# Spreading a transformer's seam products over more PSUM banks, and taking cross attention's scores a head ahead

## Chip, cores and metric

The kernel runs on one core of a Trainium2 chip, whose TensorE (PE) multiplies matrices into eight PSUM banks of 128 partitions by 512 float32 columns; VectorE (DVE), ScalarE (ACT) and GpSimd (POOL) do the rest, and SyncE (SP) issues most loads. The metric is device microseconds (us) of one execution.

## What is computed

Two transformer blocks are run one after the other on x of 512 tokens by 1024 features, all in float32. The change touches only the second, which has two layers and a last norm:

```python
for l in range(DEPTH_2):                       # 2
    h = _rmsnorm(x, g_mix[l])
    (a_cq, a_ckv, a_kr, b_q, b_ff, b_fb, b_i, b_g,
     c_q, c_k, c_v, gate_a, gate_b, gate_c) = _split_cols(h @ w_in[l], IN_SPLITS_2)
    y_a = _mla(a_cq, a_ckv, a_kr, ...)         # 8 heads, low-rank q (384) and kv (256)
    y_b = _hgrn2(b_q, b_ff, b_fb, b_i, b_g, ...)   # gated recurrence, both directions
    y_c = _window_gqa(c_q, c_k, c_v, rel_bias, c_sink[l])
    merged = (jax.nn.sigmoid(gate_a) * (y_a @ w_br_a[l])
              + jax.nn.sigmoid(gate_b) * (y_b @ w_br_b[l])
              + jax.nn.sigmoid(gate_c) * (y_c @ w_br_c[l]))
    x = x + merged @ w_out[l]
    h = _rmsnorm(x, g_x[l])
    x = x + _cross(h, _rmsnorm(mem, g_mem[l]), x_wq[l], x_wkv[l], x_wo[l])   # 4 heads, 256 keys
    h = _rmsnorm(x, g_ffn[l])
    x = x + _swiglu(h, f_w1[l], f_w3[l], f_w2[l])   # 2816 wide
return _rmsnorm(x, g_final)
```

## The kernel before

Activations stand feature-first, 8 tiles of 128 features by 512 tokens. Each float32 product is made of three matmuls: both operands are split into a rounded part and a rest (`hi`, `lo`), and `mm3` adds hi x hi, hi x lo and lo x hi. `gemm_fm` (L390) is the common product: `wslab` (L380) loads a weight slab on SP's queue into `wraw` (two buffers), ACT writes `whi`, and POOL or DVE in turn writes `wlo` (three buffers each). Then 8 tiles of the inner dimension give 24 matmuls of 128x512 into one bank, which some instruction of DVE or ACT empties (it "evacuates" the bank): mostly a product with the row of norms, `r`. With an inner dimension of 1024 that is a product of 24 matmuls; the branches of the merge have 12, and the down projection of the feed-forward 66.

The eight banks are shared by four tags of two: g, s, t and o (`ps(tag)`, L312). A product of a tag waits until one of its two banks has been emptied. In the second half g takes all products of weights; s takes scores and the state products of the recurrence, t takes transpositions and sums over partitions, o takes outputs of attention and of the recurrence.

The order of the instructions on each engine is not that of the source: the program is built with a scheduler that runs it on a model of the engines (`TileContext(..., schedule_with_timeline_sim=True)`, L2742) and writes out, for each engine, a fixed list. It lets an instruction go ahead where its bank and its operands are free in the model. On the chip each engine goes through its list in order, and waits where an operand or a bank isn't ready.

A layer of the second half has these stages, each of which opens its own pools:

- norm: the row `rmix` (names `ssacc`, `rsv`, `rsr`, `rst` are steps of its inverse root).
- recurrence `hgrn`: `hgrn_values` makes the values `hv` in two halves of two banks, for which `rmix` is transposed to tokens; then 8 heads in two directions, each with products for q and z and a chain through state tiles (`h_S` on POOL, `h_qi`, `h_kx` and others). Its end makes a norm (`rsq`) and the branch's output, split into `ybh` and `ybl`.
- latent attention `mla`: `latent` makes two k tiles and three q tiles in `mraw`, norms them and splits them to `mlhk`, `mllk`, `mlhq`, `mllq`; then products with uk, uv and uq, the rope products `p1` and `p2`, and 8 heads, whose scores are already taken one head ahead. Output `yah`, `yal`.
- `window` attention: key `wk`, value `wvf`, four query products, 8 heads; output `ych`, `ycl`.
- 24 gate products (`gates2`, evacuated to `g2z` and stored in DRAM as `gated`) are strewn between the heads of the three branches by `beside` and `next(fill)`.
- `merge2`: the tiles of the gates are loaded (`g20`, `g21`, `g22` on SP), 8 x 3 branch products are multiplied with them, and 8 products with w_out follow.
- `cross` attention: for each of 4 heads two q products (`xq`), four score tiles with softmax, then transpositions and values; 8 products with x_wo.
- `ffn`: 22 pairs of products with f_w1 and f_w3 (`fz` is the first one's evacuation), then 8 products with f_w2.

The numbers behind a name (`ps_g_18632`) in the lists of the section on the change are serial numbers of the tiles; they are the same in both kernels. The functions that the diff touches, with the profile's line numbers:

## Time and profile before

| | us |
|---|---|
| median of 3 runs | 4423.25 (4420.15 to 4430.96) |
| the profiled execution | 4420.88, of which its span 4419.1 |
| first block | up to 1823 |
| layer 0: recurrence, latent attention | 1836 to 2161, to 2361 |
| layer 0: window, merge, cross, feed-forward | to 2494, 2616, 2740, 3111 |
| layer 1: recurrence, latent attention | 3111 to 3457, to 3658 |
| layer 1: window, merge, cross, feed-forward | to 3791, 3913, 4037, 4396 |
| last norm | to 4419 |

The bounds of the stages are read from the timeline, where the first product of the next stage begins. The span is cut into windows at such bounds, and each window tells how long every engine was busy in it and which clock the throttle granted to PE (1.00 is full speed, 2.4 GHz; 0.50 is 1.2 GHz). What a window has beyond PE's busy time is PE's idle time; the waits then say which engine's instruction ended that.

### The profile page before, as it was taken

The page shows a single profiled execution, that of the slowest core. Times are in us where ns is not written, and L with a number is a line of the kernel's source. Part 1 is how long each engine was busy: PE and PEld are TensorE (multiplying, and loading weights), DVE is VectorE, ACT ScalarE, POOL GpSimd, SP SyncE. Part 2 cuts the span into 40 slices and gives each one's busy share as a digit, 9 for nine tenths or more (in the row PEclk, how much of TensorE's full clock was granted, in tenths as well). Part 3 has the DMA queues.
Part 4 walks back from the last instruction along what each step waited for, and adds up shares of the span by engine and source line. Part 5 has one row for each costly group of instructions (what it writes and reads, how often), then busy time and mean ns, then how long its engine had stood idle before and what let it go on. Part 6 is the DMA issues. An engine that isn't in the chain of part 4 may idle for free. (4 is left out here: it accounts for less than half of the span.)

```text
span 4419.1 us, 55886 instructions
## 1 busy us (share of the span) xinstructions
PE 4036.6 (91%) x20436; PEld 3236.0 (73%) x20436; DVE 2728.1 (62%) x4770; ACT 2114.6 (48%) x3424; POOL 1692.5 (38%) x1144
## 2 busy tenths in 40 slices
PE   6999799869987989799899999999999899999998
PEld 4887676658866767678676777888777677777886
DVE  6657777677655778576566655332587475665542
ACT  4565668733332768433365544442344365444432
POOL 3342676523222353233254422332344264423431
PEclk8999899979978999899999999999999899999999
DMA  4432210034215889312131332223212122422232
GB/s 154 161 123 70 91 39 8 8 130 146 82 63 186 322 315 376 117 59 70 54 109 66 112 125 71 96 91 98 73 58 75 60 86 79 134 96 81 96 92 80
DMA packets 179605, 480.55 MB, mean 109 GB/s; under 512 B 17576, under 2 KB 28904, under 8 KB 178944
## 3 DMA queue, kind: packets, MB, share of 16 engines
q1 hardware_dynamic: 172512, 452.79, 30.0%
q0 software_dynamic: 6816, 24.15, 1.6%
q8 instruction: 163, 2.67, 0.2%
q14 instruction: 114, 0.93, 0.1%
HBM read 433.31 MB, written 41.44 MB: 107 GB/s over the span
## 5 line engine op out<-in xcount | busy, mean ns | idle before, releaser
L377 POOL TENSOR_TENSOR wlo<-wraw,whi 128x1024 fp32r<-128x1024 f32 (+4 forms) x244 | 554.9, 2274 | 1172.9 <-ACT whi L329 1118.0
L329 ACT ACTIVATE whi<-wraw 128x1024 fp32r<-128x1024 f32 (+4 forms) x489 | 481.7, 986 | 934.6 <-PE ps_g L317 746.6
L317 PE MATMUL ps_g<-ha,whi 128*128 128x512 f32 x2184 | 884.6, 405 | 48.3 <-DVE mraw L357 22.8
L317 PE MATMUL ps_g<-hl,whi 128*128 128x512 f32 x2184 | 887.5, 407 | 0.0
L317 PE MATMUL ps_g<-ha,wlo 128*128 128x512 f32 x2184 | 878.6, 403 | 0.0
L317 PEld LDWEIGHTS ps_g<-ha,whi 128*128 128x128 f32 x2184 | 417.5, 191 | 157.7 <-DVE mraw L357 22.3
L317 PEld LDWEIGHTS ps_g<-ha,wlo 128*128 128x128 f32 x2184 | 417.0, 191 | 100.2 <-issue 5.0
L317 PEld LDWEIGHTS ps_g<-hl,whi 128*128 128x128 f32 x2184 | 417.7, 191 | 97.6 <-issue 5.3
L377 DVE TENSOR_TENSOR wlo<-wraw,whi 128x1024 fp32r<-128x1024 f32 (+4 forms) x245 | 296.1, 1208 | 205.3 <-ACT whi L329 198.6
L353 DVE TENSOR_TENSOR_SCAN aa<-aa 128x774 f32<-128x774 f32 x64 | 126.1, 1971 | 51.1 <-ACT aa L329 46.8
L317 PE MATMUL ps_g<-fah,wlo 128*128 128x512 f32 x352 | 137.0, 389 | 0.0
L317 PE MATMUL ps_g<-fal,whi 128*128 128x512 f32 x352 | 137.0, 389 | 0.0
L317 PE MATMUL ps_g<-fah,whi 128*128 128x512 f32 x352 | 136.9, 389 | 0.0
L367 DVE SCALAR_TENSOR_TENSOR h_R<-h_R,h_gd,ps_s 128x64 f32<-128x64 f32 x448 | 124.7, 278 | 11.9
L329 ACT ACTIVATE aa<-ps_x,aM 128x512 f32<-128x512 f32 x128 | 110.8, 949 | 33.1 <-PE ps_x L317 21.0
L317 PE MATMUL ps_g<-mlo,xh 128*128 128x512 f32 x272 | 111.4, 409 | 14.2 <-POOL mlo L1946 14.2
L2347 POOL TENSOR_SCALAR mP<-mP,sfst 128x512 f32<-128x512 f32 x64 | 102.5, 1609 | 52.6 <-DVE sfst L2346 41.7
L2561 POOL TENSOR_SCALAR g2z<-g2z 128x512 f32<-128x512 f32 x48 | 81.9, 1706 | 95.0 <-DVE g2z L357 82.3
L1517 POOL TENSOR_TENSOR dnl<-dnn,dnc 128x512 f32<-128x512 f32 x48 | 67.1, 1408 | 125.6 <-PE ps_t L317 84.6
L329 ACT ACTIVATE g2z<-g2z 128x512 f32<-128x512 f32 x144 | 90.4, 628 | 49.7 <-POOL g2z L2561 48.1
L329 ACT ACTIVATE mhi<-mrawa 128x2048 fp32r<-128x2048 f32 x52 | 99.6, 1915 | 30.0 <-PE ps_g L317 11.2
L357 DVE TENSOR_TENSOR mlo<-mrawb,mhi 128x2048 fp32r<-128x2048 f32 x42 | 102.8, 2470 | 15.6 <-ACT mhi L329 15.6
(988 smaller groups left out, 10183.8 us busy)
## 6 DMA issues: line engine op xcount, KB each, us to landing
wraw<-w_fm SPq DMA_DIRECT2D x169, 512.0 KB, 3.4
wraw<-f_w SPq DMA_DIRECT2D x120, 512.0 KB, 3.5
mrawa<-moe_g SPq DMA_DIRECT2D x18, 1024.0 KB, 10.6
mrawb<-moe_d SPq DMA_DIRECT2D x18, 1024.0 KB, 8.3
adaw<-ada_w SPq DMA_DIRECT2D x64, 256.0 KB, 3.1
mrawa<-moe_u SPq DMA_DIRECT2D x16, 1024.0 KB, 9.3
mrawb<-moe_u SPq DMA_DIRECT2D x16, 1024.0 KB, 10.5
mrawb<-moe_g SPq DMA_DIRECT2D x14, 1024.0 KB, 10.4
```

Of the source, the lines that this page charges most:

```text
L317: self.nc.tensor.matmul(out, a, b, start=start, stop=stop)
L329: return self.nc.scalar.activation(out, in_, f, **kw)
L353: return self.nc.vector.tensor_tensor_scan(out, *args, **kw)
L357: return self.nc.vector.tensor_tensor(out, a, b, op=op)
L367: return self.nc.vector.scalar_tensor_tensor(out, a, s, b, op0=op0, op1=op1)
L377: e.tensor_tensor(lo, src, hi, op=OP.subtract)
L1517: nc.gpsimd.tensor_tensor(nl, n_, dnc[:, 1 + lv, None, :].to_broadcast([128, 4, 128]), op=OP.mult)
L2347: nc.gpsimd.tensor_scalar(P, P, st[:, 3:4], None, op0=OP.mult)
L2561: self.nc.gpsimd.tensor_scalar(z, z, ZMIN, None, op0=OP.max)
```

## The change

The tag of the products at the stages' seams is given by hand. `hgrn_values`: the second half of the values on s for g. `mla`: the k and q tiles of the latents on s, g, o in turn; uk, uv and uq products on g and s in turn; the two rope products on o. `window`: key and value on s, queries on g and s in turn. `merge2`: the three branches on g, s and t, w_out on g and s in turn. `ffn`: products with f_w3 on s, those with f_w2 on g and o in turn. In `cross` a head's q products, scores and softmax become a function, which is called for the next head ahead of a head's transpositions and values. No instruction is taken out or put in, except that one row of PE's list is split; the scheduler writes a new order for every engine.

```diff
--- before.py
+++ after.py
@@ -2166,7 +2166,7 @@
         rt = self.rows(T, r, 4, "rtok")
         v = T.tile([128, 4, 512], F32, name="hv")
         for hf in range(2):
-            pa = [self.ps("g"), self.ps("g")]
+            pa = [self.ps("gs"[hf]), self.ps("gs"[hf])]
             for c in range(2):
                 hi, lo = self.wslab(self.I["w2_i%d" % l][hf * 2 + c])
                 for kk in range(4):
@@ -2385,7 +2385,7 @@
                 def latent(n, at, gname, kt):
                     raw = T.tile([128, 3, S], F32, name="mraw", bufs=1)
                     for k in range(kt):
-                        self.tt(raw[:, k, :], self.gemm_fm(W2[at + k], self.ha, self.hl), r, OP.mult)
+                        self.tt(raw[:, k, :], self.gemm_fm(W2[at + k], self.ha, self.hl, tag="sgo"[k]), r, OP.mult)
                     yield 0.5
                     rs = self.rstd_x(T, raw, S, kt)
                     yield 0.5
@@ -2407,21 +2407,21 @@
                 self.tt(t[0:32], t[0:32], ropek[0:32], OP.mult)
                 self.tt(kr, t[0:32], t2, OP.add)
                 for n in range(4):
-                    self.act(kn[:, n, :], self.gemm_fm(I["a_uk%d" % l][n], kh, kl))
+                    self.act(kn[:, n, :], self.gemm_fm(I["a_uk%d" % l][n], kh, kl, tag="gs"[n % 2]))
                 yield 0
                 hi, lo = self.wslab(I["a_uv%d" % l])
                 for b in range(4):
-                    p = self.ps("g")
+                    p = self.ps("gs"[b % 2])
                     tk = slice(b * 128, b * 128 + 128)
                     for k in range(2):
                         self.mm3(p, kh[:, k, tk], kl[:, k, tk], hi[:, k, :], lo[:, k, :], k == 0, k == 1)
                     self.act(v[:, b, :], p)
                 yield 0
                 for n in range(4):
-                    self.act(qn[:, n, :], self.gemm_fm(I["a_uq%d" % l][n], qh, ql))
+                    self.act(qn[:, n, :], self.gemm_fm(I["a_uq%d" % l][n], qh, ql, tag="gs"[n % 2]))
                 yield 0
-                p1 = self.gemm_fm(I["a_uq%d" % l][4], qh, ql)
-                p2 = self.gemm_fm(I["a_uq%d" % l][5], qh, ql)
+                p1 = self.gemm_fm(I["a_uq%d" % l][4], qh, ql, tag="o")
+                p2 = self.gemm_fm(I["a_uq%d" % l][5], qh, ql, tag="o")
                 C, Sn = rope[:, 0, :], rope[:, 1, :]
                 tm = T.tile([128, 3, S], F32, name="mraw", bufs=1)
                 for i, (x, y, op) in enumerate(((C, Sn, OP.subtract), (Sn, C, OP.add))):
@@ -2488,8 +2488,8 @@
             kn = T.tile([128, S], F32, name="wk")
             vf = T.tile([128, S], F32, name="wvf")
             v = T.tile([128, 2, 4, 128], F32R, name="wv")
-            self.tt(kn, self.gemm_fm(W2[38], self.ha, self.hl), r, OP.mult)
-            self.tt(vf, self.gemm_fm(W2[39], self.ha, self.hl), r, OP.mult)
+            self.tt(kn, self.gemm_fm(W2[38], self.ha, self.hl, tag="s"), r, OP.mult)
+            self.tt(vf, self.gemm_fm(W2[39], self.ha, self.hl, tag="s"), r, OP.mult)
             yield 0
             p = self.ps("t")
             for b in range(4):
@@ -2497,7 +2497,7 @@
             o = v.rearrange("p g b d -> p b g d")
             self.split(o[:, :, :, 0:64], o[:, :, :, 64:128], p.rearrange("p (b g d) -> p b g d", b=4, g=2))
             for i in range(4):
-                self.stt(qn[:, i, :], self.gemm_fm(W2[34 + i], self.ha, self.hl), 0.125, r, OP.mult, OP.mult)
+                self.stt(qn[:, i, :], self.gemm_fm(W2[34 + i], self.ha, self.hl, tag="gs"[i % 2]), 0.125, r, OP.mult, OP.mult)
             yield 0
             khh = T.tile([128, 2, S], F32R, name="wkhh")
             kll = T.tile([128, 2, S], F32R, name="wkll")
@@ -2585,13 +2585,13 @@
                     gs.append(T.tile([128, S], F32, name="g2%d" % br, bufs=2))
                     self.nc.sync.dma_start(gs[br], self.gated[8 * br + n])
                 for br, y in enumerate((self.ya, self.yb, self.yc)):
-                    p = self.gemm_fm(I["w2_br%d" % l][n][:, 4 * br:4 * br + 4, :], y[0], y[1])
+                    p = self.gemm_fm(I["w2_br%d" % l][n][:, 4 * br:4 * br + 4, :], y[0], y[1], tag="gst"[br])
                     self.tt(gs[br], gs[br], p, OP.mult)
                 self.nc.gpsimd.tensor_tensor(gs[0], gs[0], gs[1], op=OP.add)
                 self.tt(gs[0], gs[0], gs[2], OP.add)
                 self.split(mh[:, n, :], ml[:, n, :], gs[0])
             for n in range(8):
-                p = self.gemm_fm(I["w2_out%d" % l][n], mh, ml)
+                p = self.gemm_fm(I["w2_out%d" % l][n], mh, ml, tag="gs"[n % 2])
                 self.tt(self.x[:, n, :], p, self.x[:, n, :], OP.add)
 
     def mixer2(self, l):
@@ -2638,7 +2638,7 @@
                     c = slice(j * 256, (j + 1) * 256)
                     nc.sync.dma_start(t, self.kvd[l][1][:, :, c])
                     self.split(vh[:, :, c], vl[:, :, c], t)
-                for h in range(4):
+                def scores(h):
                     qh = T.tile([128, 2, S], F32R, name="xqh", bufs=2)
                     ql = T.tile([128, 2, S], F32R, name="xql", bufs=2)
                     for j in range(2):
@@ -2655,11 +2655,18 @@
                         for j in range(2):
                             self.mm3(o, qh[:, j, c], ql[:, j, c], kh[:, 2 * h + j, :], kl[:, 2 * h + j, :], j == 0, j == 1)
                         self.soft(T, o, 256, P[:, qi, :], 1.0)
+                    return P
+
+                P = scores(0)
+                for h in range(4):
+                    now = P
+                    if h < 3:
+                        P = scores(h + 1)
                     pts = []
                     for kt in range(2):
                         pt = self.ps("t")
                         for qi in range(4):
-                            self.tr(pt[:, qi * 128:(qi + 1) * 128], P[:, qi, kt * 128:(kt + 1) * 128])
+                            self.tr(pt[:, qi * 128:(qi + 1) * 128], now[:, qi, kt * 128:(kt + 1) * 128])
                         ph = T.tile([128, S], F32R, name="xph", bufs=4)
                         pl = T.tile([128, S], F32R, name="xpl", bufs=4)
                         self.split(ph, pl, pt)
@@ -2690,11 +2697,11 @@
                     s = self.sigmoid(T, z, [128, S], "ff", bufs=2)
                     nc.gpsimd.tensor_tensor(z, z, r, op=OP.mult)
                     self.tt(z, z, s, OP.mult)
-                    p3 = self.gemm_fm(I["f_w3%d" % l][n], self.ha, self.hl)
+                    p3 = self.gemm_fm(I["f_w3%d" % l][n], self.ha, self.hl, tag="s")
                     self.tt(z, z, p3, OP.mult)
                     self.split(ah[:, n, :], al[:, n, :], z)
             for n in range(8):
-                p = self.ps("g")
+                p = self.ps("go"[n % 2])
                 for c in range(3):
                     k0, k1 = (0, 8, 16, 22)[c:c + 2]
                     hi, lo = self.wslab(I["f_w2%d" % l][n][:, k0:k1, :])
```

Three places in the order. The first is PE at the end of layer 0's recurrence, where latent attention begins. There `h_qi` with `h_S` are the recurrence's last products with its state, the product with `rsq` is its norm, 18469 and 18632 are gate products, 18388 and 18420 the latent k tiles, 18516, 18548 and 18580 the latent q tiles; `ha` and `hl` are the normed input. Before:

```order
L317 MATMUL ps_o_17595<-h_qi_18016,h_S_18033 64x32 x8
L317 MATMUL ps_o_17595<-hps3_15631,hv_15647 64x128 x4
L317 MATMUL ps_o_17595<-h_qi_18202,h_S_18219 64x32 x15
L317 MATMUL ps_t_18343<-rsq_18341,cst_61 128x512
L317 MATMUL ps_g_18469<-ha_71,whi_18465 128x512
L317 MATMUL ps_g_18469<-hl_72,whi_18465 128x512
```

After, further ahead in the tail:

```order
L317 MATMUL ps_s_18388<-ha_71,wlo_18385 128x512
L317 MATMUL ps_o_17595<-h_qi_18202,h_S_18219 64x32 x7
L317 MATMUL ps_s_18388<-ha_71,whi_18384 128x512
L317 MATMUL ps_s_18388<-hl_72,whi_18384 128x512
L317 MATMUL ps_s_18388<-ha_71,wlo_18385 128x512
L317 MATMUL ps_s_18516<-ha_71,whi_18512 128x512
L317 MATMUL ps_s_18516<-hl_72,whi_18512 128x512
L317 MATMUL ps_s_18516<-ha_71,wlo_18513 128x512
L317 MATMUL ps_s_18516<-ha_71,whi_18512 128x512
L317 MATMUL ps_o_17595<-h_qi_18202,h_S_18219 64x32 x8
L317 MATMUL ps_s_18516<-hl_72,whi_18512 128x512
```

and at its end:

```order
L317 MATMUL ps_s_18516<-hl_72,whi_18512 128x512
L317 MATMUL ps_s_18516<-ha_71,wlo_18513 128x512
L317 MATMUL ps_t_18343<-rsq_18341,cst_61 128x512
L317 MATMUL ps_g_18632<-ha_71,whi_18628 128x512
L317 MATMUL ps_g_18632<-hl_72,whi_18628 128x512
```

Before, the first product behind `rsq` is a gate, and 18388 and 18420 are the last ahead of it in g. Now 18469, 18548, 18580, 18388 and 18516 stand ahead of `rsq`, mixed with the recurrence's last products, and the product behind `rsq` is the gate 18632, on g, where 18420 and 18548 are.

The second is PE where layer 0's window attention ends (`avh`, `avl` with `wv` are its last values) and the merge begins: 21520 and 21590 are products of the branch c, with `ych` and `ycl`, for the first and the second output tile. Before:

```order
L317 MATMUL ps_o_21416<-avl_21443,wv_20098 128x256
L317 MATMUL ps_o_21416<-avh_21451,wv_20098 128x256
L317 MATMUL ps_o_21416<-avl_21452,wv_20098 128x256
L317 MATMUL ps_g_21520<-ych_20090,whi_21516 128x512
L317 MATMUL ps_g_21520<-ycl_20091,whi_21516 128x512
L317 MATMUL ps_g_21520<-ych_20090,wlo_21517 128x512
```

After:

```order
L317 MATMUL ps_t_21520<-ych_20090,whi_21516 128x512
L317 MATMUL ps_t_21520<-ycl_20091,whi_21516 128x512
L317 MATMUL ps_t_21520<-ych_20090,wlo_21517 128x512
L317 MATMUL ps_o_21416<-avh_21451,wv_20098 128x256
L317 MATMUL ps_o_21416<-avl_21452,wv_20098 128x256
L317 MATMUL ps_t_21590<-ych_20090,whi_21586 128x512
L317 MATMUL ps_t_21590<-ycl_20091,whi_21586 128x512
L317 MATMUL ps_t_21590<-ych_20090,wlo_21587 128x512
```

Before, nothing stands between the last values and 21520, on g. Now 21520 and 21590 are on t, nine matmuls of 21520 stand ahead of the last values and nine of 21590 behind them, ahead of the rest of both.

The third is PE at the start of layer 0's feed-forward, where the second product (23395) ends and the third (23429) begins. Before:

```order
L317 MATMUL ps_g_23395<-ha_71,whi_23391 128x512
L317 MATMUL ps_g_23395<-hl_72,whi_23391 128x512
L317 MATMUL ps_g_23395<-ha_71,wlo_23392 128x512
L317 MATMUL ps_g_23429<-ha_71,whi_23425 128x512
L317 MATMUL ps_g_23429<-hl_72,whi_23425 128x512
L317 MATMUL ps_g_23429<-ha_71,wlo_23426 128x512
```

After:

```order
L317 MATMUL ps_s_23395<-ha_71,whi_23391 128x512
L317 MATMUL ps_s_23395<-hl_72,whi_23391 128x512
L317 MATMUL ps_s_23395<-ha_71,wlo_23392 128x512
L317 MATMUL ps_g_23429<-ha_71,whi_23425 128x512
L317 MATMUL ps_g_23429<-hl_72,whi_23425 128x512
L317 MATMUL ps_g_23429<-ha_71,wlo_23426 128x512
```

The order is the same there, but 23395 is on s, so that 23429 follows 23355 in g and not 23395.

## Rows read from the trace of the kernel before

**Rows 1.** The page, part 1: busy us, share of the span, instructions.

```profile
PE 4036.6 (91%) x20436; PEld 3236.0 (73%) x20436; DVE 2728.1 (62%) x4770; ACT 2114.6 (48%) x3424; POOL 1692.5 (38%) x1144
```

**Rows 2.** Windows: length, busy us (count) by engine, clock, DMA share, GB/s.

```profile
1836.00:4396.00 2560.00, 2454.73 (x11742) 1968.81 (x11742) 1443.99 (x2631) 1102.99 (x1883) 950.02 (x579) 0.98 0.26 85
2740.00:3111.00 371.00, 367.51 (x1636) 299.90 (x1634) 131.78 (x169) 135.53 (x175) 112.82 (x63) 1.00 0.29 96
```

**Rows 3.** Waits of PE, 1836 to 4396: total us, times, longest.

```profile
PE ps_g L317 <- DVE mraw L357: 22.8, 4, 7.7
PE ps_g L317 <- DVE wk L357: 6.8, 2, 3.4
PE ps_g L317 <- DVE g L357: 6.8, 2, 3.4
PE ps_g L317 <- DVE fz L357: 5.7, 2, 3.5
PE ps_g L317 <- DVE xq L367: 5.7, 2, 3.5
PE ps_t L317 <- ACT rmix L329: 5.0, 1, 5.0
PE ps_g L317 <- DVE hv L362: 3.0, 4, 1.2
```

**Rows 4.** Low-clock windows: behind rmix, hv; behind mraw, and its first; behind g, fz.

```profile
sum 13.60, PE 10.47 PEld 10.29 DVE 7.29 ACT 0.80 POOL 0.01; mean PE 5.24 PEld 5.14 DVE 3.65 ACT 0.40 POOL 0.00
sum 47.90, PE 27.64 PEld 19.59 DVE 14.48 ACT 15.08 POOL 4.28; mean PE 6.91 PEld 4.90 DVE 3.62 ACT 3.77 POOL 1.07
2155.00:2175.50 20.50, 10.19 (x33) 7.13 (x34) 5.49 (x9) 5.60 (x9) 1.04 (x1) 0.50 0.00 1
sum 17.10, PE 15.09 PEld 11.93 DVE 5.14 ACT 3.00 POOL 5.26; mean PE 5.03 PEld 3.98 DVE 1.71 ACT 1.00 POOL 1.75
```

**Rows 5.** Timeline of PE, feed-forward's start in layer 0: start, us, engine, work [idle].

```profile
2743.83 0.50 PE L317 MATMUL ps_g<-ha,whi 128*128 128x512 f32 x1 [3.49 <-DVE fz L357]
2744.41 0.39 PE L317 MATMUL ps_g<-ha,wlo 128*128 128x512 f32 x1
2744.64 0.39 PE L317 MATMUL ps_g<-ha,whi 128*128 128x512 f32 x1
```

**Rows 6.** Timeline of PE, start of layer 1's recurrence.

```profile
3116.15 1.96 PE L317 MATMUL ps_t<-cst,rmix 1*128 1x64 f32 x8 [4.98 <-ACT rmix L329]
3119.66 0.42 PE L317 MATMUL ps_g<-wlo,ha 128*128 128x256 f32 x1
3119.88 0.41 PE L317 MATMUL ps_g<-whi,hl 128*128 128x256 f32 x1
```

**Rows 7.** Windows: tails, seams, prologues of both layers; heads of layer 0.

```profile
2138.20:2161.60 23.40, 17.51 (x149) 13.74 (x147) 11.79 (x39) 3.27 (x6) 5.00 (x5) 0.86 0.15 51
2161.60:2169.30 7.70, 0.00 (x0) 0.00 (x1) 4.18 (x7) 3.20 (x5) 0.00 (x0) 0.50 0.00 0
2169.30:2239.10 69.80, 63.80 (x250) 49.93 (x251) 29.17 (x40) 31.62 (x53) 17.27 (x10) 0.93 0.22 71
2239.10:2363.30 124.20, 115.69 (x528) 89.83 (x528) 88.52 (x183) 86.09 (x170) 79.92 (x46) 0.97 0.25 83
3433.30:3456.70 23.40, 17.42 (x141) 13.11 (x139) 11.60 (x33) 4.05 (x7) 6.32 (x5) 0.90 0.17 51
3456.70:3464.40 7.70, 0.01 (x1) 0.01 (x1) 4.18 (x7) 3.23 (x6) 0.00 (x0) 0.50 0.00 0
3464.40:3535.40 71.00, 64.60 (x250) 50.20 (x250) 31.39 (x40) 32.33 (x54) 16.46 (x10) 0.92 0.22 70
```

**Rows 8.** Timeline, latent attention's start in layer 0.

```profile
2169.30 0.79 PE L317 MATMUL ps_g<-ha,whi 128*128 128x512 f32 x1 [7.71 <-DVE mraw L357]
2177.58 1.02 PE L317 MATMUL ps_t<-ssacc,cst 128*128 128x512 f32 x2
2186.47 1.29 DVE L357 TENSOR_TENSOR mllk<-mraw,mlhk 128x512 fp32r<-128x512 f32 x2
```

## The prediction

> **What bounds the kernel now.** I read the page's busy shares first: TensorE (PE) is busy for 91% of the span, the next engine for 62% [rows 1]. The change takes no matmul away, so it can only give back time in which PE stands idle or runs at the lower of its two clock levels (1.2 GHz, a granted clock of 0.50). The windows come next: the two layers of the second half, 1836 to 4396 us, hold 2454.73 us of PE work in 2560.00, so 105.3 us are idle; layer 0's feed-forward alone is busy for 367.51 of 371 us at clock 1.00 [rows 2]. The waits of PE say for whom it stands, and the large ones each lie where one stage ends and the next begins [rows 3]: the new stage's products take banks of tag g, both are full, and VectorE (DVE), which works in order, empties them only behind the last steps of the ended stage. Last I looked at the clock behind such a wait: it is 0.50 for some microseconds, and what is busy there takes twice its time, so half of it is lost [rows 4]. At full clock a 128x512 matmul is started every 0.23 us (2744.41, 2744.64) [rows 5], so a product of 24 is 5.5 us.
>
> **The change, part by part.** Instructions, loads and their sizes stay; banks, order and waits change. Each part is worth the idle time and the half-clock loss that go, less what comes anew. The sum is made against the profiled execution, 4420.88 us (span 4419.1, and 1.8 around it); the median shown is 4423.25, 2.4 more, which I add at the end.
>
> *A, values of the recurrence.* The second half of the values goes to tag s, so its matmuls stand ahead of the transposition of rmix: 67 in layer 1, 14 in layer 0. Layer 1 waits 4.98 us on rmix [rows 6] and up to 1.2 on hv behind it, layer 0 up to 1.2 on hv [rows 3]. A 128x256 matmul is started every 0.22 us at half clock (3119.66, 3119.88) [rows 6], so every 0.11 at full: 67 are 7.4 us and outlast 6.2, 14 are 1.5 and outlast 1.2. The work at half clock behind both waits is 10.47, 5.2 lost [rows 4]. Saved: 5.0 + 1.2 + 1.2 + 5.2 = 12.6. The s banks are next wanted by the first head's state products; if these now wait for hv, 1.2 per layer come back and half of the clock's part: low end 7.
>
> *B, recurrence to latent attention, the largest part and the least certain.* Layer 0: the recurrence's tail is idle for 23.40 - 17.51 = 5.9 us, the wait of the next product is 7.7, and the prologue up to the rope products is idle for 69.80 - 63.80 = 6.0; layer 1: 6.0, 7.7 and 6.4 [rows 7]. That is 19.6 and 20.1. After, one gate product and the three latent q products (96 matmuls, 22 us) stand in the tail and cover its 5.9; their weight loads come earlier on SP's queue, whose engines are 0.15 busy there [rows 7], so I cost that at nothing (were they late, the cover is gone and 5.9 comes back). But the first product behind the transposed rsq still takes a g bank, and both are held by products that leave through mraw on DVE, the releaser of the wait of before [rows 8]: 7.7 stays in layer 0, and in layer 1 ten matmuls of an s product stand in between, 5.4. Then cover has been spent. From the sum of squares (2177.58) to mllk (2186.47 + 1.29) the latent k chain takes 9.2 us behind its last matmul [rows 8]; four products stood beside it, 27 matmuls (6.2) do now: 2.5 to 3 bare. The latent q chain has the same steps with three tiles for two, and 20 matmuls (4.6) stand beside it: 4.6 bare at least, and I take 4.5, since its first tile is enough to start the next product. The last waits on mraw, 22.8 - 2 x 7.7 = 7.4 over both layers [rows 3], go, since the rope products get tag o. After: 7.7 + 2.5 + 4.5 = 14.7 and 5.4 + 7.0 = 12.4. Saved 4.9 + 7.7 = 12.6. The half-clock work is 27.64, 13.8 lost [rows 4]; waits of the same size remain, so I leave that. Bounds: 0 (both chains come bare by what the tails give) and 30 (the seam's wait halves and half of 13.8 goes).
>
> *C, heads of latent attention, and the seam to the window.* Four window products move into the last two heads, gate products leave the middle ones. The product behind still waits for wk on DVE: 6.8 stays [rows 3]. The heads are idle for 124.20 - 115.69 = 8.5 in layer 0 [rows 7]. I take 2 for both layers, nearer to nothing than to 8.5, since filling only moves; bounds -8 and 8.
>
> *D, window to merge.* Two merge products on g and s and one more on s move into the window's last heads, and behind its last value matmuls 9 matmuls of a second t product and 6 remaining ones stand ahead of the next g product: 15 x 0.23 = 3.4 us against the 3.4 per layer now waited for g [rows 3]. Saved 6.8 with what the tail gives. Price: the pulled products' slabs are loaded on SP ahead of the gate tiles g; the g evacuation waits for these, and behind it PE's next product and all of the merge. If the loads came late by one slab, 3 us per layer would be back: low end 1.
>
> *E, cross attention.* The next head's scores stand ahead of a head's values. The third q product still waits for xq, 5.7 [rows 3], and inside the stage a q product of 5.5 us already covered the softmax. If that cover were gone, a head would show its softmax chain bare, some 2 us. 0, bounds -4 and 3.
>
> *F, feed-forward.* w1 and w3 products alternate between g and s, so the third no longer waits for fz: 3.49 in layer 0 [rows 5], 5.7 over both [rows 3]. The half-clock work of D and F together is 15.09, 7.5 lost [rows 4]. f_w2 on g and o at nothing: a product is 66 matmuls, 15 us, beside an evacuation of some 0.65 (as mllk's tiles [rows 8]); without that cover it is 0.65 x 8.
>
> D, F and their clock: 6.8 + 5.7 + 7.5 = 20.0. Sum: 12.6 + 12.6 + 2 + 0 + 20.0 = 47.2; 4420.88 - 47.2 = 4373.7, with 2.4 for the median **4376**.
>
> **The rivals.** *Rival 1: the banks are full again.* DVE, not the bank, sets the seams, so only the plain idle of A, D and F goes (7.4 + 6.8 + 5.7 = 19.9) and clock, B and C give nothing: 4401, at the median 4403. For it: wk, xq and the 7.7 on mraw keep their place in the new order. Against it: in A and F a bank is free where none was. Chance 0.15.
>
> *Rival 2: all seams fill.* The seven waits [rows 3], 55.8, the two tails, 11.9, and half of all the listed half-clock work (10.47 + 27.64 + 15.09, so 26.6 [rows 4]) go: 94, so 4327, at the median 4329. Against it: three of the waits have the same releaser in the new order. Chance 0.08. The Trainium skill, "Perfetto Trace Analysis", Matmul Optimizations, asks to make use of all 8 PSUM banks so that more instructions can go on at once; by that rule it would be this rival.
>
> *Rival 3: cover is spent, and the kernel is slower.* Both latent chains come wholly bare, 9.2 each [rows 8], with half of 10.19 at low clock behind each, as behind the wait of 7.7 [rows 4]: 28.6 per layer, 57.2 in all. The gains of A, D, F with their clock (32.6) and of the rope products (7.4) stand against it: +17.2, at the median 4440. It decides from 20 us per layer. For it: four of the five products between the seam and the k chain's end have been moved ahead. Against it: gate, uk and uv products still stand there. Chance 0.06.
>
> *Rival 4: banks in turn make short idles.* If each of the 22 pairs of feed-forward products in two layers brought one stretch of 3.4 us at clock 0.50, 44 x 1.7 = 75 are lost against the whole gain of 47: +28, at the median 4451. Against it: before, the same products alternate between two banks at clock 1.00 [rows 2], and more banks give more time, not less. Chance 0.03. The Trainium skill, "TensorE: Matmul & The Clock Gate", A second HAM failure mode: psum-queue depth-cycling, tells of a kernel that cycled through banks at each iteration and whose clock swung between the two levels through short idles; no row here shows that.
>
> **How the numbers follow.** Forecast 0.63, with the bounds of B, C and D between 4350 and 4400; rival 1 0.15, rival 2 0.08, rival 3 0.06, rival 4 0.03, and 0.05 for mixtures around 4410 to 4425. The range 4350 to 4405 holds the forecast and rival 1. Two runs of this kernel tell a difference from about 0.3%, 13 us. Faster: forecast, rival 2 and nearly all of rival 1, 0.85; within: the mixtures and a part of rival 1, 0.07; slower: rivals 3 and 4, 0.08.
>
> **What would show it.** In the waits after: rmix, hv and fz gone from the seams, g down to about nothing, wk and xq as before, mraw from 22.8 to about 13 (7.7 + 5.4), and new waits of 2 to 5 us on mlhk, mllk, mlhq or mllq. In the windows: the feed-forward shorter by about 5 in layer 0, idle time of the whole stretch near 70. Wrong are B if mraw's long wait is gone or the new ones exceed 7 per layer, D if PE waits for g behind late loads, F if its clock falls below 1.00 inside the stage.

## The result: 48 us less, against 47 forecast

| | before | after |
|---|---|---|
| median us | 4424.07 (4420.15 to 4430.96) | 4374.84 (4374.02 to 4376.81) |
| profiled execution, its span | 4420.88, 4419.1 | 4374.36, 4372.6 |

The ratio of the times is 0.9891, with a 95% interval of 0.9878 to 0.9903: 43 to 54 us less. Forecast were 4376, a range of 4350 to 4405, and faster by 0.3% or more with a chance of 0.85.

The page of the changed kernel (busy us, share of the span, instructions) answers to [rows 1]:

```profile
PE 4022.2 (92%) x20436; PEld 3226.2 (74%) x20436; DVE 2722.7 (62%) x4770; ACT 2113.4 (48%) x3424; POOL 1687.8 (39%) x1144
```

As many matmuls as before, and 14.4 us less busy time for them: that is work which had run at half clock. The rest of the 46.5 us of span is idle time. The windows of the two layers and of layer 0's feed-forward, cut at the same work as in [rows 2]:

```profile
1837.70:4349.50 2511.80, 2438.05 (x11736) 1954.99 (x11734) 1438.27 (x2632) 1101.60 (x1884) 946.78 (x579) 0.99 0.26 87
2726.84:3094.09 367.25, 367.25 (x1639) 300.34 (x1637) 133.24 (x169) 135.18 (x175) 112.95 (x63) 1.00 0.29 97
```

In the two layers 2511.80 - 2438.05 = 73.8 us are idle where 105.3 were, and layer 0's feed-forward is never idle. The waits of PE (total us, times, longest), as [rows 3]:

```profile
PE ps_g L317 <- DVE mraw L357: 14.8, 2, 8.3
PE ps_s L317 <- ACT mP L329: 7.9, 15, 1.7
PE ps_s L317 <- DVE wk L357: 7.0, 2, 3.6
PE ps_g L317 <- ACT mlhq L329: 6.8, 2, 3.8
PE ps_g L317 <- DVE xq L367: 5.7, 2, 3.5
PE ps_g L317 <- DVE g L357: 3.9, 2, 2.5
PE ps_o L317 <- POOL h_S L2314: 2.8, 2, 1.8
```

Waits on rmix, hv and fz are gone; wk and xq stand where they stood, in total 7.0 and 5.7. Of mraw's four waits the two long ones are left, 14.8 of 22.8. New is 6.8 on mlhq; 3.9 are left of 6.8 on g; and mP has grown to 7.9 from this line of the kernel before:

```profile
PE ps_s L317 <- ACT mP L329: 4.3, 8, 1.3
```

### The profile page after: what moved, and what is told of

Its sections match the earlier page's. It is cut to its first block, busy times and chain, and to the rows that moved or that the text cites. A ratio compares the mean times of both kernels' runs of the same rounds, so it can differ in the third digit from the quotient of the medians.

```text
span 4372.6 us, 55762 instructions
## 1 busy us (share of the span) xinstructions
PE 4022.2 (92%) x20436; PEld 3226.2 (74%) x20436; DVE 2722.7 (62%) x4770; ACT 2113.4 (48%) x3424; POOL 1687.8 (39%) x1144
## 5 line engine op out<-in xcount | busy, mean ns | idle before, releaser
L317 PE MATMUL ps_g<-ha,whi 128*128 128x512 f32 x1720 | 699.2, 407 | 31.5 <-DVE mraw L357 14.8
L317 PE MATMUL ps_g<-hl,whi 128*128 128x512 f32 x1720 | 698.0, 406 | 0.0
L317 PE MATMUL ps_g<-ha,wlo 128*128 128x512 f32 x1720 | 691.9, 403 | 0.5 <-POOL wlo L377 0.4
L317 PEld LDWEIGHTS ps_g<-ha,whi 128*128 128x128 f32 x1720 | 328.0, 191 | 112.6 <-DVE mraw L357 16.0
L317 PEld LDWEIGHTS ps_g<-ha,wlo 128*128 128x128 f32 x1720 | 327.7, 191 | 80.2 <-issue 4.0
L317 PEld LDWEIGHTS ps_g<-hl,whi 128*128 128x128 f32 x1720 | 328.1, 191 | 76.3 <-issue 5.6
L317 PE MATMUL ps_s<-ha,whi 128*128 128x512 f32 x448 | 179.1, 400 | 7.8 <-DVE wk L357 7.0
L317 PE MATMUL ps_s<-hl,whi 128*128 128x512 f32 x448 | 180.8, 404 | 0.0
L317 PE MATMUL ps_s<-ha,wlo 128*128 128x512 f32 x448 | 177.9, 397 | 0.0
L329 ACT ACTIVATE mhi<-mrawa 128x2048 fp32r<-128x2048 f32 x52 | 99.6, 1914 | 30.7 <-PE ps_g L317 11.7
L329 ACT ACTIVATE mhi<-mrawb 128x2048 fp32r<-128x2048 f32 x50 | 95.7, 1914 | 34.4 <-PE ps_g L317 22.0
```

Source lines behind the costliest of these rows:

```text
L317: self.nc.tensor.matmul(out, a, b, start=start, stop=stop)
L329: return self.nc.scalar.activation(out, in_, f, **kw)
```

## What each part gave

For each stretch of the trace I took PE's idle time and half of what was busy at a granted clock of 0.50, before and after; the difference is the part's gain. Beside it stand the forecast and, where the part was run alone, its gain on the chip (its ratio times 4421 us, with the interval).

| part | forecast | in the trace of the whole | alone, on the chip |
|---|---|---|---|
| A, values | 12.6 | 12.9 | 9.7 (5 to 15) |
| B, recurrence to latent attention | 12.6 | 19.1 (13.9 idle, 5.2 clock) | 14.6 (10 to 19) |
| C, heads, seam to the window | 2 | -2.1 | 3.1 (-1 to 7), window tags |
| D, merge | 12.6 | 9.9 | 14.6 (9 to 20) |
| E, cross attention | 0 | -0.8 | 2.7 (-2 to 7) |
| F, feed-forward | 7.4 | 7.4 | 3.5 (0 to 8) |
| sum | 47.2 | 46.4 | 48 |

The single parts add to what all of them give, within their intervals. Three rows of the table are not as forecast, B, C and D, and their errors cancel: +6.5, -4.1 and -2.7. The column from the trace is one execution of each kernel, and its clock part moves by some us from one to the next: in the second profile of the changed kernel (it is run again below) no low clock follows the merge's seam in layer 0, and D has 1.6 us more.

## Experiments

### One part at a time

Each kernel is the one before with the edits of one part, as the diff of the change has them. A alone:

```diff
-            pa = [self.ps("g"), self.ps("g")]
+            pa = [self.ps("gs"[hf]), self.ps("gs"[hf])]
```

> The kernel before with one edit: the second half of the recurrence's values on bank tag s. Theory (the seam's idle time goes and with it the low clock behind it): 12.6 us less than before, as part A was counted; no wait of PE on rmix in layer 1 and none on hv over 0.3. Rival (the clock stays low, only idle time goes): 7.4 less. Rival (the parts are not separate, since the scheduler writes the whole order anew): anything else, below 5 or above 18.

Measured: 4411.75 (ratio 0.9978, 0.9967 to 0.9989), 9.7 us less by the ratio. In its trace PE has no wait on rmix and none on hv. Idle time and low clock fall from 9.7 to 0 us in layer 1, so the seam's wait is gone and not moved. The interval, 5 to 15, can't tell 12.6 from the 7.4 without the clock; the trace has both parts gone.

B alone, all tags of `mla`:

```diff
-    self.gemm_fm(W2[at + k], self.ha, self.hl)
+    self.gemm_fm(W2[at + k], self.ha, self.hl, tag="sgo"[k])
...
-    p1 = self.gemm_fm(I["a_uq%d" % l][4], qh, ql)
+    p1 = self.gemm_fm(I["a_uq%d" % l][4], qh, ql, tag="o")
```

> The kernel before with the edits of latent attention alone (latent tiles on s, g, o; uk, uv, uq on g and s; rope products on o). Theory: the recurrence's tail is filled and the rope products' wait goes, the long wait on mraw stays at 6 to 8.3 per layer; 12.6 us less by the sum of the prediction, 19 if the low clock at the tail goes too, as the trace after shows. Rival (cover is spent): 0 or slower, with waits over 9 us on mlhk or mlhq. Rival (all of this gain comes from the rope products): 7.4.

Measured: 4409.56 (0.9967, 0.9957 to 0.9977), 14.6 us less by the ratio, 10 to 19: the sum's 12.6 lies inside, 19 at its edge, and both rivals outside. And its rope products alone, that is only the last two lines above and their like for `p2`:

> The kernel before with the two rope products on tag o, nothing else. Theory (of latent attention's gain of 14.6 us this is the wait of 4.1 and 3.3, and the filled tail the rest): 7.4 to 9 less, the waits of 7.7 on mraw as before. Rival (it is all of that gain): 13 to 15 less.

Measured: 4410.12 (0.9971, 0.9959 to 0.9982), 12.8 us less by the ratio, between the theory and the rival: the rope products alone bring nearly all that latent attention's edits bring. The waits of the two (total, times, longest), first with the rope products alone:

```profile
PE ps_g L317 <- DVE mraw L357: 15.4, 2, 7.7
PE ps_o L317 <- POOL h_S L2314: 8.5, 6, 1.8
```

and with all of latent attention:

```profile
PE ps_g L317 <- DVE mraw L357: 14.8, 2, 8.3
PE ps_g L317 <- ACT mlhq L329: 7.0, 2, 3.9
PE ps_o L317 <- POOL h_S L2314: 2.8, 2, 1.8
```

With all edits a third of h_S's waits is left (2.8 of 8.5, the recurrence's tail), but mlhq has 7.0 of its own. Where the rest went is seen in the windows of the heads, layer 0 and layer 1 (length, busy us of each engine, clock, DMA share, GB/s). Rope products alone:

```profile
2239.00:2370.50 131.50, 120.93 (x544) 91.84 (x543) 93.69 (x192) 89.42 (x176) 81.34 (x46) 0.97 0.24 78
3530.80:3665.00 134.20, 124.27 (x566) 95.35 (x565) 97.10 (x196) 92.34 (x179) 80.06 (x46) 0.97 0.25 77
```

All of latent attention:

```profile
2238.00:2374.70 136.70, 125.05 (x552) 96.29 (x552) 98.26 (x192) 89.33 (x176) 79.13 (x46) 0.94 0.25 80
3534.00:3668.00 134.00, 122.44 (x542) 94.45 (x541) 97.26 (x190) 87.42 (x175) 81.50 (x46) 0.94 0.25 78
```

The heads are idle for 131.50 - 120.93 = 10.6 and 134.20 - 124.27 = 9.9 with the rope products alone, and for 11.7 and 11.6 with all edits; their clock is 0.97 in the one and 0.94 in the other. The clock decides nothing: with cross attention's edits alone, which leave these stages as they were, the stretch from behind the rope products to the window's values has a clock of 0.93 in both layers, where the kernel before has 0.95 and 0.96 for the same 552 matmuls.

What fills the tail can be counted. Products with `ha` and `hl`, the gates and the latent tiles above all, need nothing of the chains beside them; they are the filling. Between the product with rsq and the end of the rope products there are 144 such matmuls per layer with the rope products alone, and 48 and 58 with all edits; ahead of rsq there are as many more (742 and 731 become 838 and 817), and in the heads there are 260 in the one and 260 and 262 in the other. So the tail is filled from latent attention's own start, and not from the heads. Idle time of both layers ahead of rsq, from the recurrence's first head on, falls from 20.8 to 9.1 us; from there to the end of the rope products it rises from 20.4 to 25.0, and from there to the window's values from 20.8 to 25.0. So three quarters of what the tail gains is given back behind it; why the heads have a part in that, with the same filling, is open.

These are single executions, and the two medians differ by less than their intervals; that filling the tail alone is worth nothing is therefore likely and not shown. Shown is that 7.4 of idle time on the rope products was worth some 12 (8 to 18). A low clock behind that wait, which the prediction's part B did not count, is a part of it: in layer 0 of the kernel before 3.40 us of work at 0.50 stand behind it, from 2240.4 on, and none with the rope products alone.

D alone:

```diff
-    p = self.gemm_fm(I["w2_br%d" % l][n][:, 4 * br:4 * br + 4, :], y[0], y[1])
+    p = self.gemm_fm(I["w2_br%d" % l][n][:, 4 * br:4 * br + 4, :], y[0], y[1], tag="gst"[br])
...
-    p = self.gemm_fm(I["w2_out%d" % l][n], mh, ml)
+    p = self.gemm_fm(I["w2_out%d" % l][n], mh, ml, tag="gs"[n % 2])
```

> The kernel before with the edits of the merge alone (branches on g, s, t; w_out on g and s). Theory: in the trace after PE still waits for g, because DVE makes a weight rest (wlo) ahead of the g evacuation and waits for its slab; so about 10 us less and not 12.6, and a wait of PE on g of 1 to 3 us per layer. Rival (the full bank was all): 12.6 less and no wait on g. Rival (the gate loads come late): under 5 less.

Measured: 4408.66 (0.9967, 0.9954 to 0.9979), 14.6 us less by the ratio and 12.4 by the medians, with a wait on g of 3.9 as in the whole. So the wait is the edit's own; late loads, under 5, are out by the time, and the full bank as the whole cause by the wait. The interval, 9 to 20, can't tell 10 from 12.6.

F alone:

```diff
-    p3 = self.gemm_fm(I["f_w3%d" % l][n], self.ha, self.hl)
+    p3 = self.gemm_fm(I["f_w3%d" % l][n], self.ha, self.hl, tag="s")
...
-    p = self.ps("g")
+    p = self.ps("go"[n % 2])
```

> The kernel before with the edits of the feed-forward alone (w3 products on s, w2 products on g and o). Theory: 7.4 us less, no wait of PE on fz, clock 1.00 inside the stage. Rival (banks in turn make short idles and the clock falls): slower, with stretches at clock 0.50 inside the stage. Rival (the third product only waits elsewhere): 0.

Measured: 4417.92 (0.9992, 0.9982 to 1.0001). The gain of 7.4 lies at the edge of 0 to 8 us, and 0 at the other. In the trace fz has no wait, and the window of layer 0's feed-forward (length, busy us of each engine, clock) has no idle time and full clock, so banks in turn make no short idles here (the window begins 1.7 us ahead of the first product):

```profile
2728.80:3102.30 373.50, 373.50 (x1637) 303.90 (x1636) 133.03 (x171) 137.29 (x177) 112.31 (x62) 1.00 0.31 97
```

E alone, `scores(h)` as in the change:

```diff
-                for h in range(4):
+                def scores(h):
...
+                P = scores(0)
+                for h in range(4):
+                    now = P
+                    if h < 3:
+                        P = scores(h + 1)
```

> The kernel before with cross attention's scores taken ahead, nothing else. Theory: 0, between 3 less and 2 more; the wait for xq stays at 5.7. Rival (the changed order covers the softmax and the seam): 5 or more less. Rival (values are pushed back and the products with x_wo wait): 3 or more slower.

Measured: 4421.10 (0.9994, 0.9985 to 1.0004), so nothing that can be told from 0; the wait on xq is 5.7 as before.

The window alone:

```diff
-    self.tt(kn, self.gemm_fm(W2[38], self.ha, self.hl), r, OP.mult)
+    self.tt(kn, self.gemm_fm(W2[38], self.ha, self.hl, tag="s"), r, OP.mult)
...
-    self.stt(qn[:, i, :], self.gemm_fm(W2[34 + i], self.ha, self.hl), 0.125, r, OP.mult, OP.mult)
+    self.stt(qn[:, i, :], self.gemm_fm(W2[34 + i], self.ha, self.hl, tag="gs"[i % 2]), 0.125, r, OP.mult, OP.mult)
```

> The kernel before with the window's tags alone. Theory: the wait on wk stays at 6.8 and the filling moves within the heads: between 4 less and 3 more; so that C's loss in the changed kernel comes from the gates that latent attention's edit pulled out of the heads. Rival (C's loss is the window's own): 3 or more slower.

Measured: 4422.44 (0.9993, 0.9984 to 1.0002): nothing, and the wait on wk is 7.4, where it was 6.8. Waits on mP are 8.2 here too, while those on avl and avh fall from 14.7 to 8.7, so that mP by itself tells nothing. The idle time from behind the rope products to the window's values does (sums over both layers: length, busy us of each engine); in order the kernel before, latent attention's edits alone, the window's alone, and the changed kernel:

```profile
sum 266.70, PE 246.09 PEld 190.91 DVE 187.15 ACT 175.47 POOL 157.15; mean PE 123.04 PEld 95.45 DVE 93.57 ACT 87.74 POOL 78.58
sum 276.10, PE 251.11 PEld 193.18 DVE 200.90 ACT 178.71 POOL 163.18; mean PE 125.56 PEld 96.59 DVE 100.45 ACT 89.36 POOL 81.59
sum 285.10, PE 266.81 PEld 207.87 DVE 194.44 ACT 183.19 POOL 161.79; mean PE 133.40 PEld 103.94 DVE 97.22 ACT 91.60 POOL 80.90
sum 293.20, PE 268.64 PEld 208.27 DVE 206.41 ACT 185.46 POOL 167.65; mean PE 134.32 PEld 104.13 DVE 103.20 ACT 92.73 POOL 83.83
```

That is 20.6, 25.0, 18.3 and 24.6 us idle, and 19.9 to 21.7 in the four kernels with other parts edited; the last two windows hold some 48 matmuls more per layer, of the window's products. So the window's tags do not make C's loss, and latent attention's edits do.

### The waits that stayed

The changed kernel itself was run again beside the next three.

> The changed kernel once more, beside the three that follow. Theory (the four parts of the first experiments add): 45 to 50 us less than before. Rival (its first result owed some of it to the chip it ran on): under 40.

Measured: 4375.71 against 4421.09 before (0.9898, 0.9882 to 0.9915), 45 us less, as the parts add. What the new order left at the seam of the recurrence is seen in PE's timeline of the changed kernel, layer 0 (start, us, engine, work, [idle before and what ended it]):

```profile
2183.35 0.80 PE L317 MATMUL ps_g<-ha,whi 128*128 128x512 f32 x1 [8.31 <-DVE mraw L357]
2192.77 0.50 PE L317 MATMUL ps_g<-ha,whi 128*128 128x512 f32 x1 [0.78 <-DVE g2z L357]
2214.78 0.75 PE L317 MATMUL ps_g<-mlhq,whi 128*128 128x512 f32 x1 [3.80 <-ACT mlhq L329]
2231.03 0.51 PE L317 MATMUL ps_g<-ha,whi 128*128 128x512 f32 x1 [1.59 <-ACT whi L329]
```

The first row is the wait that [rows 8] has as 7.71: the gate 18632 finds both g banks held by latent products until DVE has made mraw. One gate was therefore put on another tag, so that in the written order other products stand behind rsq:

```diff
-            p = self.gemm_fm(self.I["w2_fm%d" % l][40 + i], self.ha, self.hl)
+            p = self.gemm_fm(self.I["w2_fm%d" % l][40 + i], self.ha, self.hl, tag="t" if i in (5,) else "g")
```

> The changed kernel with the sixth gate product on bank tag t for g, so that at the recurrence's end the products behind the transposed rsq find a free bank: 46 matmuls, 10.6 us, stand there instead of the gate that waits for mraw. Theory (that wait, 8.3 and 6.5 us, is a full bank): no wait on mraw over 1 us, and 12 to 18 us less than the changed kernel, the low clock behind it with it. Rival (the work that fills it is taken from the tail, which comes bare): 3 to 7 less, with 5 us idle again ahead of rsq per layer. Rival (the chain on DVE sets the end and the wait moves to the latent k products): 0 to 3 less, with waits on mlhk of 5 us or more.

Measured: 4353.97 (4352.07 to 4360.87), ratio 0.9854 (0.9837 to 0.9871): 21.7 us less than the changed kernel by the medians and 19.5 by the two ratios, above all that was expected. The window of the seam and the prologue in layer 0 (length, busy us of each engine, clock):

```profile
2161.00:2240.00 79.00, 74.49 (x310) 57.40 (x309) 45.05 (x61) 42.64 (x72) 20.54 (x13) 1.00 0.29 86
```

It is idle for 4.5 us, and its clock is 1.00; the wait on mraw isn't among PE's waits any more, and none on mlhq. So the wait was a bank, not the chain: nothing else came late by more than 1.7 us. Idle time and clock loss of B fall from 20.0 and 15.9 us (the changed kernel beside it) to 7.8 and 4.4, 23.7 in all. The first rival is there in small: 118 and 123 matmuls of filling stand behind rsq again (48 and 58 in the changed kernel), idle time there falls from 24.2 to 5.1 us over both layers, and ahead of rsq, where they are missing, it rises from 8.0 to 14.0.

For D, the timeline of DVE, ACT and PE at the merge's start in the changed kernel:

```profile
2490.58 0.69 DVE L357 TENSOR_TENSOR ycl<-wy,ych 128x512 fp32r<-128x512 f32 x1 [0.70 <-ACT ych L329]
2491.86 1.15 ACT L329 ACTIVATE whi<-wraw 128x512 fp32r<-128x512 f32 x2 [1.32 <-PE ps_t L317]
2493.05 1.34 DVE L377 TENSOR_TENSOR wlo<-wraw,whi 128x512 fp32r<-128x512 f32 x1 [1.78 <-ACT whi L329]
2494.31 0.67 DVE L357 TENSOR_TENSOR g<-g,ps_g 128x512 f32<-128x512 f32 x1
2495.04 0.80 PE L317 MATMUL ps_g<-yah,whi 128*128 128x512 f32 x1 [2.50 <-DVE g L357]
```

The g evacuation, for which PE waits, could run when ycl is done (2491.3). DVE comes to it at 2494.31, since its list has a weight's rest (wlo) in front, which waits for ACT's whi, and that for a buffer which the ych products on t hold. Before, g followed ycl at once:

```profile
2495.74 0.69 DVE L357 TENSOR_TENSOR ycl<-wy,ych 128x512 fp32r<-128x512 f32 x1 [0.69 <-ACT ych L329]
2496.35 1.28 DVE L357 TENSOR_TENSOR g<-g,ps_g 128x512 f32<-128x512 f32 x2
```

The edit makes all the rests of the merge on POOL:

```diff
         I = self.I
+        self.lo_pool = self.lo_of
         with self.pool("mg2") as T:
...
+        self.lo_pool = 1
```

> The changed kernel with the rests of the merge's weights (wlo) all made by POOL instead of by POOL and DVE in turn. Theory (at the merge's start the g evacuation stands on DVE behind a wlo that waits for a weight slab): PE's wait on g goes from 3.9 us over both layers to under 1.5, and 2 to 5 us less than the changed kernel. Rival (the gate tiles' loads are late): the wait on g stays at 3.9, 0 less. Rival (POOL becomes late with the rests, 1.3 us each): new waits on wlo, slower.

Measured: 4376.07 (0.9900, 0.9884 to 0.9917), the same as the changed kernel beside it. Its waits:

```profile
PE ps_g L317 <- DVE mraw L357: 14.8, 2, 8.3
PE ps_s L317 <- DVE wk L357: 7.0, 2, 3.6
PE ps_g L317 <- POOL wlo L377: 3.4, 4, 1.4
PE ps_t L317 <- POOL wlo L377: 1.0, 2, 0.5
```

No wait on g is left, so the cause is shown: DVE's list. But 4.4 us of waits on POOL's wlo have come (0.6 in the changed kernel), and nothing is won. The wait was moved, as the second rival had it, though not to a slower kernel.

All seams at once: both edits, and

```diff
-    p = self.gemm_fm(I["x_wq%d" % l][2 * h + j], self.ha, self.hl)
+    p = self.gemm_fm(I["x_wq%d" % l][2 * h + j], self.ha, self.hl, tag="go"[j])
...
-    self.stt(qn[:, i, :], self.gemm_fm(W2[34 + i], self.ha, self.hl, tag="gs"[i % 2]), 0.125, r, OP.mult, OP.mult)
+    self.stt(qn[:, i, :], self.gemm_fm(W2[34 + i], self.ha, self.hl, tag="go"[i % 2]), 0.125, r, OP.mult, OP.mult)
```

> The changed kernel with both of these, and with cross attention's q products on g and o in turn and the window's query products on g and o in turn, so that the products that wait for xq and wk find a free bank. Theory (each seam's wait is a full bank, and covers add): waits on mraw, wk, xq and g together from 31 us to under 6, half of the low clock behind them with them; 30 to 43 us less than the changed kernel. Rival (filling is only moved, and heads and chains come bare instead): under 20 less, with the waits on mP, avl, avh and mlhq up by 10 or more.

Measured: 4356.46 (0.9851, 0.9833 to 0.9868), no better than the gate alone. The waits on mraw, wk, xq and g are all gone, and these are the longest that are left:

```profile
PE ps_o L317 <- DVE avl L357: 7.8, 10, 2.0
PE ps_s L317 <- ACT mP L329: 6.7, 11, 2.1
PE ps_t L317 <- DVE h_qi L367: 5.8, 6, 1.7
PE ps_s L317 <- ACT xP L329: 5.2, 5, 2.1
PE ps_g L317 <- POOL wlo L377: 4.0, 4, 1.7
```

Those on avl and mP are not new (6.5 and 7.9 in the changed kernel), h_qi had 4.7 with the gate alone; xP and wlo are. In cross attention the softmax (xP, 5.2) takes the place of xq (5.7): in the written order more of the q products stand ahead of the first scores (in layer 0 91 matmuls, 74 in the next kernel, which has cross attention as before this edit). Of the theory the waits came true and the gain did not; of the rival the time did, but not its waits: mP, avl, avh and mlhq together are 16.9, where the changed kernel has 25.3. What the two edits cost is seen where merge and cross attention lie, from the window's last value to cross attention's end, over both layers. The sums (length, busy us of each engine) of this kernel, of the gate alone, and of the next kernel:

```profile
sum 456.30, PE 439.12 PEld 348.76 DVE 267.58 ACT 179.04 POOL 176.59; mean PE 219.56 PEld 174.38 DVE 133.79 ACT 89.52 POOL 88.30
sum 448.20, PE 435.19 PEld 353.78 DVE 270.08 ACT 181.04 POOL 138.53; mean PE 217.60 PEld 176.89 DVE 135.04 ACT 90.52 POOL 69.27
sum 445.40, PE 432.38 PEld 351.66 DVE 273.00 ACT 180.55 POOL 136.06; mean PE 216.19 PEld 175.83 DVE 136.50 ACT 90.27 POOL 68.03
```

For the same matmuls these stages are 8 to 11 us longer with the two edits. At the window it is otherwise: idle time from behind the rope products to the window's values falls from 24.2 us over both layers with the gate alone to 18.2. So the last kernel has the gate and the window's queries alone.

> The changed kernel with the sixth gate on t and the window's query products on g and o in turn, without the edits of cross attention and merge. Theory (wk's wait is a full bank too, and in the run with all four edits the cross edit gave its gain back as waits on xP and the merge edit its gain as waits on wlo): 5 to 10 us less than with the gate alone, so 4344 to 4349, no wait on wk over 1 us. Rival (the heads come bare by what the seam gains): the same as with the gate alone, 4351 to 4357.

Measured: 4340.39 (4337.00 to 4345.46), ratio 0.9812 (0.9799 to 0.9825): the fastest of all, 1.9% below the kernel before, and 13.6 below the gate alone by the medians of two sets of runs, where 5 to 10 were expected. The two spans, 4350.9 and 4336.4, differ by 14.5, and 4.9 of that lie in the first block, which no edit touches (the norm behind it begins at 1827.7 in the one and 1822.7 in the other); behind it 9.6 are left, as expected. Idle time from behind the rope products to the window's values is 16.9, from 24.2. Among its waits are

```profile
PE ps_o L317 <- DVE avl L357: 6.8, 10, 1.9
PE ps_s L317 <- ACT mP L329: 6.6, 10, 2.1
PE ps_g L317 <- DVE xq L367: 5.7, 2, 3.5
PE ps_g L317 <- DVE g L357: 3.9, 2, 2.5
```

with none on wk and none on mraw.

## Why the prediction held, step by step

**A and F** were sized right: 12.9 and 7.4 in the trace against 12.6 and 7.4. In both a bank was free, the cover was counted by matmuls and their rate, and the clock behind the wait was taken from rows. Two readings were a little off. Half of the work at low clock was counted as lost; in the trace before a 128x512 matmul is started every 0.43 us behind mraw's wait (2169.89, 2170.32, 2170.74) and every 0.23 at full clock, so 0.46 is nearer. And layer 0's feed-forward was to be shorter by about 5 and is by 3.75, since before no low clock followed its wait; the clock's part lies in layer 1.

**B**: the order's main reading was right. The wait on mraw stays, 8.31 and 6.45 where 7.7 and 5.4 were written; the tail is filled; the rope products' wait goes; the q chain comes bare by 3.80 and 3.01, where 4.5 was taken. The k chain's 2.5 didn't show: 0.78 and 0.88 on a gate's evacuation took its place. Idle time fell by 13.9, 12.6 were forecast. The step that failed is "waits of the same size remain, so I leave that": the low-clock work fell from 27.64 us [rows 4] to

```profile
sum 27.30, PE 17.15 PEld 12.92 DVE 14.51 ACT 6.96 POOL 0.00; mean PE 4.29 PEld 3.23 DVE 3.63 ACT 1.74 POOL 0.00
```

17.15 us in four stretches, so 5.2 came in addition. The tail itself had been low in clock from 2155.0 on [rows 4], ahead of the wait, and filling it kept it at full clock up to 2177.3.

**C** was given +2 and is -2.1. The step "filling only moves" was right and its sign not: filling was taken forward within the heads. Ahead of the fourth, fifth and sixth head's scores there were 105 and 90 matmuls of it (layer 0 and 1) and are 48 and 62, and PE's idle time there grew from 0.9 to 6.5 us. That the one makes the other is argued, since no run put the filling back. Within the bounds of -8 and 8.

**D** was given 12.6 and is 9.9. The step that failed is "15 x 0.23 = 3.4 us against the 3.4 per layer": the cover was held against the old wait, as if DVE would still come to g right after ycl. The pulled products hold the weights' buffers longer, and a rest that waits for one stands ahead of g in DVE's list, so 3.9 of wait on g remain. The price named, late gate loads, wasn't it. Of the 2.7 missing, 1.6 came back in the second profile of the same kernel, so by one trace the miss can't be sized closer.

**E** was right: 0, and xq stays at 5.7.

**Rival 1** (only idle time goes, 4403) falls with the clock's part in A, B, D and F: 14.4 us less busy time for the same matmuls. **Rival 2** (4329) is not the change's, but the gate's tag and the last kernel show that 4354 and 4340 are to be had from the same eight banks. The Trainium skill ("Perfetto Trace Analysis", Matmul Optimizations) asks to use all of them; that agrees with the gate's and the window's tags, and not with those of cross attention's q products, where the waits went from xq (5.7) to xP (5.2). **Rival 3** (cover is spent) is there on a small scale, as mlhq's 6.8 and the heads' loss. **Rival 4** (short idles) isn't seen: the feed-forward with banks in turn is busy for all of 367.25 us at clock 1.00.

So the sum was nearer than its parts, and that is luck: the errors of B, C and D cancel, and by their size a miss of 5 to 10 us would have been no surprise.

## What to carry to other kernels

Before a bank is given to a seam, find in the written order which product comes first behind the seam and who must empty the bank that it takes: here one gate's tag (21.7 us) was worth more than any single part of the change, for the same banks. Filling that is pulled ahead into one gap is missing in the next; count it in the written order before and after, as with the recurrence's tail and latent attention's start behind it, or with the heads. And look in the queue of the engine that evacuates for what stands in front of the evacuation: a wait that goes from there may only change its engine. Before two single profiles are compared, take off what they differ by in stages that no edit touches.

## What the runs showed that was not expected

The wait of 3.49 us ahead of layer 0's third feed-forward product was not followed by a low clock in the execution of [rows 5] (0.39 us for a matmul behind it), while one of 2.16 in layer 1 was. In the profile of the rope products alone the same wait of 3.5 is followed by it; the low stretch, which begins within the wait (length, busy us of each engine, clock):

```profile
2738.50:2745.30 6.80, 5.46 (x13) 4.29 (x14) 3.79 (x6) 2.74 (x5) 1.28 (x1) 0.50 0.39 133
```

Here 5.46 us of work took twice its time. So the price of a wait in clock varies from run to run, and it is a part of the scatter. The first block shows how much that can be: its matmuls are the same in all kernels, and the norm behind it begins between 1822.7 us (the gate with the window's queries) and 1833.1 (the merge's edits alone), where half of the work at 0.50 is 91 and 102 us. The kernel before took 4413.74 to 4430.96 us over all runs, with granted clocks of 0.946 to 0.952, the changed one 4374.02 to 4377.29, at 0.950 to 0.954.
